# Sliding windows of 64 rows at stride 32: which blocks go through SBUF, and which ring moves the rest

## The chip, the cores and the metric

One core of a Trainium2 chip. The time is that of one execution on the device, in microseconds; every kernel was run several times and the median of its runs is given. A profile of an execution was taken as well; its span is some 2 us shorter than the time of the same execution.

## The reference, cut to what matters

```python
batch, length, dim = (32, 4096, 256)          # float32
window_size, stride = 64, 32
n_windows = (length - window_size) // stride + 1          # 127
for i in range(n_windows):
    start = i * stride
    result[:, i] = x[:, start:start + window_size]
```

Nothing is computed. A block is 32 rows of 256 floats, 32 KB; a batch has 128 blocks, and window w is blocks w and w+1. So each block is written twice, as the second half of one window and the first half of the next, except the first and the last of a batch. Input 134.2 MB, output 266.3 MB.

## The kernel before

There are two ways to fill the output. A *direct* copy goes from the input to the output, both in HBM: every output byte passes the DMA engines once, and is read from HBM and written to it. A *staged* block is loaded into SBUF once and stored from there twice: three passes of the engines for two output blocks, but one HBM read in place of two (the page's HBM line below bears this out). The kernel stages 11 of the 32 batches on the ACT ring, copies most of the others directly on the SP ring, 16 windows to a DMA, and leaves the edges of those to POOL's software ring, which starts when SP is nearly through. A ring is the queue of packets that one issuer (SP, ACT or POOL) fills, and the page has one queue for each. While two rings had work, the packet records count as many packets of the one as of the other: 2567 of SP's and 2574 of ACT's from 160 to 380 us in the first profile of before, whatever their sizes. One packet is called one *turn*, and a ring's turns here are its packets over 16 engines. The 4-byte packets are among them: 16 for each DMA of SP and ACT (3264 for SP's 204, 656 for ACT's 41). I take them for completions, as the trace has 16 semaphore updates for each DMA too (4272 for all 267).

```python
def windows(self, q, b, w0, n, half=None, piece=DIRECT):      # direct copy of n windows, or of one half of each
    blk = self.blk
    row = [1, 2 * blk if half is None else blk]
    h = half or 0
    return q.dma_start(out=self.oap((b * self.nw + w0) * 2 + h, [[2 * blk, n], row]),
                       in_=self.xap(b * self.nb + w0 + h, [[blk, n], row]), max_dma_last_dim=piece)
# ...
staged = [*range(1, B, 3)]                                    # 11 whole batches, 128 blocks each
# ...
edges = [(b, 0 if b - 1 in staged else 112, 15) for b in direct[:-1]]       # 20 software DMAs of 15 windows
# ...
st.run(ring_s)                                                # ACT: 6 loads, 12 stores, 5 loads, the other stores
for i, (b, w) in enumerate(sixteens):                         # SP
    sem = near if i == len(sixteens) - 2 else done
    second = turns - first_loads - stores
    loading = turns < first_loads or 0 <= second < loads
    share += 120 if turns < 16 or -8 <= second < 16 else 90 if loading else 18
    if share >= 120:                                          # "cut": one DMA for each half
        share -= 120
        turns += 4
        count(c.windows(ring_d, b, w, 16, 0), done)
        count(c.windows(ring_d, b, w, 16, 1), sem)
    else:
        turns += 3
        count(c.windows(ring_d, b, w, 16), sem)
# ...
ring_r.wait_ge(near, 16)                                      # POOL starts when SP's last copy but one has landed
```

The `share` counter decides which of SP's copies are cut into two DMAs. A cut adds 16 of the 4-byte packets, one turn more of SP's ring for the same bytes, and ACT's ring gets ahead: from 220 to 280 us ACT had 652 packets of 16 KB to SP's 442 of 32 KB in the first profile of before. This is how the kernel tunes the two rings against each other.

Of the kernel before, what the change touches and what calls it, by code (L numbers as in the profile page):

```python
# [8 lines left out]
DIRECT, IN, OUT = 32768, 16384, 16384  # L9


class Copier:


    def __init__(self, x, out, B, L, D, W, S, n_win):
        assert W == 2 * S and L % S == 0
        self.x, self.out = x, out
        self.B = B
        self.blk = S * D
        self.nb = L // S  # L20
        self.nw = n_win

    def xap(self, block, dims):
        return bass.AP(self.x.tensor, self.x.offset + block * self.blk, dims)

    def oap(self, half_window, dims):
        return bass.AP(self.out.tensor, self.out.offset + half_window * self.blk, dims)

    def windows(self, q, b, w0, n, half=None, piece=DIRECT):

        blk = self.blk
        row = [1, 2 * blk if half is None else blk]
        h = half or 0
        return q.dma_start(  # L34
            out=self.oap((b * self.nw + w0) * 2 + h, [[2 * blk, n], row]),
            in_=self.xap(b * self.nb + w0 + h, [[blk, n], row]),
            max_dma_last_dim=piece,
        )

    def columns(self, q, b, w0, n):  # L40

        part = self.blk // 8
        row = [1, part]
        return q.dma_start(  # L44
            out=self.oap((b * self.nw + w0) * 2, [[part, 16], [2 * self.blk, n], row]),
            in_=self.xap(b * self.nb + w0, [[part, 16], [self.blk, n], row]),
        )

    def load(self, q, t, b, c, rows):

        p, step, n, unit = rows
        return q.dma_start(
            out=t[p : p + (n - 1) * step + 1 : step, :],
            in_=self.xap(b * self.nb + c + p // unit, [[step // unit * self.blk, n], [1, self.blk]]),
            max_dma_last_dim=IN,
        )

    def store(self, q, t, b, c, rows, half):


        p, step, n, unit = rows
        w = b * self.nw + c + p // unit - half
        return q.dma_start(
            out=self.oap(2 * w + half, [[2 * step // unit * self.blk, n], [1, self.blk]]),
            in_=t[p : p + (n - 1) * step + 1 : step, :],
            max_dma_last_dim=OUT,
        )


class Staging:  # L70


    def __init__(self, c, tc, pool, dtype, items, bufs):
        self.c, self.items = c, items
        self.tiles = [pool.tile([128, c.blk], dtype, name=f"xb{i}") for i in range(bufs)]
        self.loaded = [tc.alloc_semaphore(f"loaded{i}") for i in range(bufs)]
        self.stored = [tc.alloc_semaphore(f"stored{i}") for i in range(bufs)]
        self.ended = tc.alloc_semaphore("ended")
        self.count = {sem: 0 for sem in (*self.loaded, *self.stored, self.ended)}
        self.after_load, self.after_store = {}, {}  # L80

    def issue(self, dma, sem):
        dma.then_inc(sem, 16)
# [1 line left out]

    def load(self, q, g):
        i = g % len(self.tiles)
        b, c, n = self.items[g]
        if self.count[self.stored[i]]:
            q.wait_ge(self.stored[i], self.count[self.stored[i]])  # L90
        step = 128 // n
        parts = [(k, 4, 32, 1) for k in range(4)] if g == 0 else [(0, step, n, step)]
        for rows in parts:
            self.issue(self.c.load(q, self.tiles[i], b, c, rows), self.loaded[i])
        self.after_load[g] = self.count[self.loaded[i]]

    def store(self, q, g):
        i = g % len(self.tiles)
        b, c, n = self.items[g]
        q.wait_ge(self.loaded[i], self.after_load[g])  # L100
        step = 128 // n
        parts, end = [((0, step, n, step), 0), ((0, step, n, step), 1)], []
        if g == len(self.items) - 1:

            parts = [((0, 1, 128, 1), 1), ((0, 1, 32, 1), 0)]
            end = [(96, 1, 32, 1)] + [(32 + k, 4, 16, 1) for k in range(4)]
        for rows, half in parts:
            self.issue(self.c.store(q, self.tiles[i], b, c, rows, half), self.stored[i])
        for rows in end:
            self.issue(self.c.store(q, self.tiles[i], b, c, rows, 0), self.ended)  # L110
        self.after_store[g] = self.count[self.stored[i]]

    def wait_stored(self, q, g):
        q.wait_ge(self.stored[g % len(self.tiles)], self.after_store[g])  # L114

    def run(self, q):
        bufs = len(self.tiles)
        for first in range(0, len(self.items), bufs):
            group = range(first, min(first + bufs, len(self.items)))
            for g in group:  # L120
                self.load(q, g)
            for g in group:
                self.store(q, g)


@with_exitstack
def kernel(
    ctx: ExitStack,
    tc: tile.TileContext,
    x: bass.AP,  # L130
    window_size: bass.AP,
    stride: bass.AP,
    out: bass.AP,
):
    nc = tc.nc
    W, S = int(window_size), int(stride)
    B, L, D = x.shape
    n_win = (L - W) // S + 1
    assert out.shape == (B, n_win, W, D)
    c = Copier(x, out, B, L, D, W, S, n_win)  # L140


    staged = [*range(1, B, 3)]
    items = [(b, -1 if b == B - 1 else 0, c.nb) for b in staged]
    place = {b: g for g, (b, _, n) in enumerate(items) if n == c.nb}
    direct = [b for b in range(B) if b not in staged]
    pool = ctx.enter_context(tc.tile_pool(name="xb", bufs=1))
    st = Staging(c, tc, pool, x.dtype, items, 6)
    ring_d, ring_s, ring_r = nc.sync, nc.scalar, nc.gpsimd
    done = tc.alloc_semaphore("done")  # L150
    near = tc.alloc_semaphore("near")
    rest = tc.alloc_semaphore("rest")
    total = {done: 0, near: 0, rest: 0}

    def count(dma, sem):
        dma.then_inc(sem, 16)
        total[sem] += 16



    sixteens = []
    for b in direct:
        w = 15 if b - 1 in staged else 0
        sixteens += [(b, w + 16 * j) for j in range((c.nw - w) // 16)]
    singles = [(B - 1, c.nw - 1, 1)]
    edges = [(b, 0 if b - 1 in staged else 112, 15) for b in direct[:-1]]
    last = B - 2
    edges.append((last, 112, 4))

    first_loads, loads, stores = 6 * 17, 5 * 17, 6 * 34  # L170
    turns = share = 0
    with tc.tile_critical():  # L172
        st.run(ring_s)

        for i, (b, w) in enumerate(sixteens):
            sem = near if i == len(sixteens) - 2 else done
            second = turns - first_loads - stores
            loading = turns < first_loads or 0 <= second < loads
            share += 120 if turns < 16 or -8 <= second < 16 else 90 if loading else 18
            if share >= 120:  # L180
                share -= 120
                turns += 4
                count(c.windows(ring_d, b, w, 16, 0), done)
                count(c.windows(ring_d, b, w, 16, 1), sem)
            else:
                turns += 3
                count(c.windows(ring_d, b, w, 16), sem)
            if i == len(sixteens) // 2:
                for b, w, half in singles:
                    count(c.windows(ring_d, b, w, 1, half, 2048), done)  # L190

        ring_r.wait_ge(near, 16)
        for b, w, n in edges:
            for k in (b - 1, b + 1):
                if k in place and b != last:
                    st.wait_stored(ring_r, place[k])
            count(c.windows(ring_r, b, w, n), rest)


        count(c.columns(ring_r, last, 116, 9), rest)  # L200
        st.wait_stored(ring_d, place[B - 1])
        count(c.columns(ring_d, last, 125, 2), done)
        total[st.ended] = st.count[st.ended]
        for sem, n in total.items():
            ring_d.wait_ge(sem, n)


# [33 lines left out]
```

## Time and profile before

| | before |
|---|---|
| median of 5 runs | 745.56 us (745.42 to 746.23) |
| span of the first profile | 749.4 us |
| span of a second profile (run e0_before, below) | 743.9 us |
| moved by the engines | 313.26 MB |

The first profile, on which the prediction rests, fell on an execution that took 751.2 us, longer than any timed one. Its page is shown in the prediction, with some of its waits (for whom: total us, times, longest); the HBM traffic, from the page: Two more lines of it matter later: the HBM traffic, from the page, and SP's last wait, from the waits of SP's queue (for whom: total us, times, longest).

```profile
HBM read 220.95 MB, written 267.09 MB: 651 GB/s over the span
```

```profile
SPq L172 <- POOLq L172: 1.7, 1, 1.7
```

A direct byte counts twice in the line, a staged one once for each pass: 174.83 MB went directly (q1 and q0), 46.14 were loaded and 92.27 stored, which makes 220.97 read and 267.10 written. The second lies at the very end: all data has landed (the last packet of the three rings ends at 745.8 us), and SP waits until POOL has finished a drain instruction (746.67 to 748.53 us in the trace).

### The profile page before, as it was taken

How to read it: one execution, taken by the hardware profiler on the slowest of the kernel's cores; microseconds unless marked ns; L12 is line 12 of the kernel's file. 1: busy time of each engine (PE TensorE's matmuls, PEld its weight loads, DVE VectorE, ACT ScalarE, POOL GpSimd, SP SyncE). 2: the span in 40 equal slices, each digit the busy share in tenths (PEclk: the TensorE clock that was granted, in tenths of full speed). 3: DMA queues.
4: the chain of work that ended last, by engine and by line, in shares of the span. 5: the costliest groups of instructions: out<-in, count | busy, mean ns of one | idle time of the engine just before them, and what ended most of it. 6: DMA issues, size and time to landing. Idle time of an engine off the chain costs nothing.

```text
span 749.4 us, 322 instructions
## 1 busy us (share of the span) xinstructions
POOL 12.8 (2%) x26
## 2 busy tenths in 40 slices
POOL 0000000000000000000000000000000000040100
DMA  8999999999999999999999999999999999999996
GB/s 360 401 427 429 427 429 428 434 423 418 420 424 423 418 424 415 422 427 427 414 427 417 429 432 429 430 422 430 429 423 421 423 421 419 425 426 423 431 409 262
DMA packets 18290, 313.26 MB, mean 418 GB/s; under 512 B 4336, under 2 KB 4336, under 8 KB 4528
## 3 DMA queue, kind: packets, MB, share of 16 engines
q1 hardware_dynamic: 8016, 154.32, 48.8%
q10 hardware_dynamic: 9104, 138.41, 44.0%
q0 software_dynamic: 1168, 20.51, 6.5%
q14 instruction: 2, 0.02, 0.0%
HBM read 220.95 MB, written 267.09 MB: 651 GB/s over the span
## 4 chain that ended last, share of the span: by engine, by line
another core or an unknown queue 92%; POOL 2%; issue 0%; POOLq 0%; SPq 0%
POOL out_dram L34 2%; POOL out_dram L44 0%; POOLq L236 0%; SPq L172 0%; POOLq L114 0%
## 5 line engine op out<-in xcount | busy, mean ns | idle before, releaser
L34 POOL DMA_DIRECT2D out_dram<-in_x_dram x21 | 12.0, 576 | 691.3 <-DMA out_dram<-in_x_dram 654.0
L44 POOL DMA_DIRECT2D out_dram<-in_x_dram x1 | 0.6, 581 | 0.0
L222 POOL MEMSET const-float32-0.0<- 128x1 f32 x1 | 0.1, 98 | 0.2 <-issue 0.2
L222 POOL MEMSET const-bfloat16-1.0<- 128x1 bf16 x1 | 0.1, 101 | 0.0
L222 POOL MEMSET const-float32-1.0<- 128x1 f32 x1 | 0.1, 98 | 0.0
L222 POOL MEMSET const-uint8-127<- 128x1 uint8 x1 | 0.1, 98 | 0.0
## 6 DMA issues: line engine op xcount, KB each, us to landing
out_dram<-in_x_dram SPq DMA_DIRECT2D x92, 1024.0 KB, 100.7
out_dram<-xb ACTq DMA_DIRECT2D x21, 4096.0 KB, 139.7
out_dram<-in_x_dram SPq DMA_DIRECT2D x110, 512.0 KB, 90.3
xb<-in_x_dram ACTq DMA_DIRECT2D x10, 4096.0 KB, 131.4
out_dram<-in_x_dram POOLq DMA_DIRECT2D x20, 960.0 KB, 38.5
xb<-in_x_dram ACTq DMA_DIRECT2D x4, 1024.0 KB, 15.7
out_dram<-xb ACTq DMA_DIRECT2D x2, 1024.0 KB, 113.4
out_dram<-xb ACTq DMA_DIRECT2D x4, 512.0 KB, 96.9
```

The source lines that it names most:

```text
L34: return q.dma_start(out=self.oap((b * self.nw + w0) * 2 + h, [[2 * blk, n], row]), in_=self.xap(b * self.nb + w0 + h, [[blk, n], row]), m ...
L44: return q.dma_start(out=self.oap((b * self.nw + w0) * 2, [[part, 16], [2 * self.blk, n], row]), in_=self.xap(b * self.nb + w0, [[part, 16 ...
L222: nc = _bacc.Bacc("TRN2", target_bir_lowering=False, num_devices=1)
```

## The change

It stages 64 inner blocks of 23 batches instead of all blocks of 11, so that no block is written twice. Two batches share a tile, on even and odd partitions. The outermost half windows next to the staged ranges go as "columns": 16 pieces of 2 KB for each of the 32 batches, one such DMA on each hardware ring. The last 14 windows of every batch go to the software ring, in DMAs of 14 or 7 windows.

```diff
-    def columns(self, q, b, w0, n):
-        part = self.blk // 8
+    def columns(self, q, b, w, half, n):
+        part = self.blk // 16
         row = [1, part]
         return q.dma_start(
-            out=self.oap((b * self.nw + w0) * 2, [[part, 16], [2 * self.blk, n], row]),
-            in_=self.xap(b * self.nb + w0, [[part, 16], [self.blk, n], row]),
+            out=self.oap(b, w, half, [[part, 16], [2 * self.nw * self.blk, n], row]),
+            in_=self.xap(b, w + half, [[part, 16], [self.nb * self.blk, n], row]),
         )
 ...
-    staged = [*range(1, B, 3)]
-    items = [(b, -1 if b == B - 1 else 0, c.nb) for b in staged]
+    far, pairs, n = B // 2, 11, 64
+    items = [(g, far, 1, n) for g in range(pairs + 1)]
+    alone = pairs
 ...
-        st.run(ring_s)
+        st.run(ring_s, lambda: count(c.columns(ring_s, 0, 0, 0, B)))     # after ACT's first 24 stores
 ...
-            share += 120 if turns < 16 or -8 <= second < 16 else 90 if loading else 18
+            share += 120 if turns < 16 or -8 <= second < 16 else 104 if loading else 83
 ...
+            if i == 84:
+                count(c.columns(ring_d, 0, n, 1, B))
         ring_r.wait_ge(near, 16)
-        for b, w, n in edges:
-            # (waits on staged stores, then a DMA of 15 windows)
+        for b in range(B):
+            w = n + 49
+            for m in (14,) if b % 2 else (7, 7):
+                c.remainder(ring_r, b, w, m).then_inc(rest, 16)
+                total_rest += 16
+                w += m
```

More of the change, by code (lines that the diff above doesn't have):

```diff
@@ L21, in __init__, with xap, oap, windows @@
         self.nw = n_win
-    def xap(self, block, dims):
-        return bass.AP(self.x.tensor, self.x.offset + block * self.blk, dims)
-    def oap(self, half_window, dims):
-        return bass.AP(self.out.tensor, self.out.offset + half_window * self.blk, dims)
-    def windows(self, q, b, w0, n, half=None, piece=DIRECT):
+    def xap(self, b, block, dims):
+        return bass.AP(self.x.tensor, self.x.offset + (b * self.nb + block) * self.blk, dims)
+    def oap(self, b, w, half, dims):
+        return bass.AP(self.out.tensor, self.out.offset + ((b * self.nw + w) * 2 + half) * self.blk, dims)
+    def windows(self, q, b, w, half=None):
         blk = self.blk
@@ L34, in windows, with remainder, load, store @@
         return q.dma_start(
-            out=self.oap((b * self.nw + w0) * 2 + h, [[2 * blk, n], row]),
-            in_=self.xap(b * self.nb + w0 + h, [[blk, n], row]),
-            max_dma_last_dim=piece,
-        )
-    def columns(self, q, b, w0, n):
-        part = self.blk // 8
+            out=self.oap(b, w, h, [[2 * blk, 16], row]),
+            in_=self.xap(b, w + h, [[blk, 16], row]),
+            max_dma_last_dim=DIRECT,
+        )
+    def remainder(self, q, b, w, n):
+        blk = self.blk
+        return q.dma_start(
+            out=self.oap(b, w, 0, [[2 * blk, n], [1, 2 * blk]]),
+            in_=self.xap(b, w, [[blk, n], [1, 2 * blk]]),
+            max_dma_last_dim=DIRECT,
+        )
+    def columns(self, q, b, w, half, n):
+        part = self.blk // 16
         row = [1, part]
         return q.dma_start(
-            out=self.oap((b * self.nw + w0) * 2, [[part, 16], [2 * self.blk, n], row]),
-            in_=self.xap(b * self.nb + w0, [[part, 16], [self.blk, n], row]),
-        )
-    def load(self, q, t, b, c, rows):
-        p, step, n, unit = rows
+            out=self.oap(b, w, half, [[part, 16], [2 * self.nw * self.blk, n], row]),
+            in_=self.xap(b, w + half, [[part, 16], [self.nb * self.blk, n], row]),
+        )
+    def load(self, q, t, b, c, k, step, n):
         return q.dma_start(
-            out=t[p : p + (n - 1) * step + 1 : step, :],
-            in_=self.xap(b * self.nb + c + p // unit, [[step // unit * self.blk, n], [1, self.blk]]),
+            out=t[k : k + (n - 1) * step + 1 : step, :],
+            in_=self.xap(b, c, [[step // 2 * self.blk, n], [1, self.blk]]),
             max_dma_last_dim=IN,
         )
-    def store(self, q, t, b, c, rows, half):
-        p, step, n, unit = rows
-        w = b * self.nw + c + p // unit - half
+    def store(self, q, t, b, c, k, n, half):
         return q.dma_start(
-            out=self.oap(2 * w + half, [[2 * step // unit * self.blk, n], [1, self.blk]]),
-            in_=t[p : p + (n - 1) * step + 1 : step, :],
+            out=self.oap(b, c - half, half, [[2 * self.blk, n], [1, self.blk]]),
+            in_=t[k : 2 * n : 2, :],
             max_dma_last_dim=OUT,
@@ L70, with __init__ @@
 class Staging:
-    def __init__(self, c, tc, pool, dtype, items, bufs):
-        self.c, self.items = c, items
+    def __init__(self, c, tc, pool, dtype, items, alone, bufs):
+        self.c, self.items, self.alone = c, items, alone
         self.tiles = [pool.tile([128, c.blk], dtype, name=f"xb{i}") for i in range(bufs)]
@@ L77, in __init__ @@
         self.stored = [tc.alloc_semaphore(f"stored{i}") for i in range(bufs)]
-        self.ended = tc.alloc_semaphore("ended")
-        self.count = {sem: 0 for sem in (*self.loaded, *self.stored, self.ended)}
-        self.after_load, self.after_store = {}, {}
+        self.count = {sem: 0 for sem in (*self.loaded, *self.stored)}
+        self.after_load = {}
     def issue(self, dma, sem):
@@ L87, in load @@
         i = g % len(self.tiles)
-        b, c, n = self.items[g]
         if self.count[self.stored[i]]:
             q.wait_ge(self.stored[i], self.count[self.stored[i]])
-        step = 128 // n
-        parts = [(k, 4, 32, 1) for k in range(4)] if g == 0 else [(0, step, n, step)]
-        for rows in parts:
-            self.issue(self.c.load(q, self.tiles[i], b, c, rows), self.loaded[i])
+        b, far, c, n = self.items[g]
+        step = 4 if g == 0 else 2
+        for k in range(step if g != self.alone else 1):
+            dma = self.c.load(q, self.tiles[i], b + far * (k % 2), c + k // 2, k, step, 2 * n // step)
+            self.issue(dma, self.loaded[i])
         self.after_load[g] = self.count[self.loaded[i]]
@@ L98, in store, with run @@
         i = g % len(self.tiles)
-        b, c, n = self.items[g]
         q.wait_ge(self.loaded[i], self.after_load[g])
-        step = 128 // n
-        parts, end = [((0, step, n, step), 0), ((0, step, n, step), 1)], []
-        if g == len(self.items) - 1:
-            parts = [((0, 1, 128, 1), 1), ((0, 1, 32, 1), 0)]
-            end = [(96, 1, 32, 1)] + [(32 + k, 4, 16, 1) for k in range(4)]
-        for rows, half in parts:
-            self.issue(self.c.store(q, self.tiles[i], b, c, rows, half), self.stored[i])
-        for rows in end:
-            self.issue(self.c.store(q, self.tiles[i], b, c, rows, 0), self.ended)
-        self.after_store[g] = self.count[self.stored[i]]
-    def wait_stored(self, q, g):
-        q.wait_ge(self.stored[g % len(self.tiles)], self.after_store[g])
-    def run(self, q):
+        b, far, c, n = self.items[g]
+        for half in (0, 1):
+            for k in (0, 1) if g != self.alone else (0,):
+                self.issue(self.c.store(q, self.tiles[i], b + far * k, c, k, n, half), self.stored[i])
+    def run(self, q, between):
         bufs = len(self.tiles)
@@ L123, in run, with wait_all @@
                 self.store(q, g)
+            if not first:
+                between()
+    def wait_all(self, q):
+        for sem in self.stored:
+            q.wait_ge(sem, self.count[sem])
 @with_exitstack
@@ L140 @@
     c = Copier(x, out, B, L, D, W, S, n_win)
-    staged = [*range(1, B, 3)]
-    items = [(b, -1 if b == B - 1 else 0, c.nb) for b in staged]
-    place = {b: g for g, (b, _, n) in enumerate(items) if n == c.nb}
-    direct = [b for b in range(B) if b not in staged]
+    far, pairs, n = B // 2, 11, 64
+    items = [(g, far, 1, n) for g in range(pairs + 1)]
+    alone = pairs
     pool = ctx.enter_context(tc.tile_pool(name="xb", bufs=1))
-    st = Staging(c, tc, pool, x.dtype, items, 6)
+    st = Staging(c, tc, pool, x.dtype, items, alone, 6)
@@ L149 @@
     ring_d, ring_s, ring_r = nc.sync, nc.scalar, nc.gpsimd
-    done = tc.alloc_semaphore("done")
     near = tc.alloc_semaphore("near")
     rest = tc.alloc_semaphore("rest")
-    total = {done: 0, near: 0, rest: 0}
-    def count(dma, sem):
-        dma.then_inc(sem, 16)
-        total[sem] += 16
-    sixteens = []
-    for b in direct:
-        w = 15 if b - 1 in staged else 0
-        sixteens += [(b, w + 16 * j) for j in range((c.nw - w) // 16)]
-    singles = [(B - 1, c.nw - 1, 1)]
-    edges = [(b, 0 if b - 1 in staged else 112, 15) for b in direct[:-1]]
@@ L167, with count @@
-    last = B - 2
-    edges.append((last, 112, 4))
-    first_loads, loads, stores = 6 * 17, 5 * 17, 6 * 34
+    total_rest = 0
+    done = tc.alloc_semaphore("done")
+    total = 0
+    def count(dma):
+        nonlocal total
+        dma.then_inc(done, 16)
+        total += 16
+    whole, split = [], []
+    for b in range(B):
+        whole += [(b, w) for w in range(n + 1, n + 49, 16)]
+        if b % far >= pairs and b != alone:
+            split += [(b, w) for w in range(0, n, 16)]
+    first_loads, loads, stores = 6 * 18, 5 * 18 + 9, 6 * 36
@@ L171 @@
     turns = share = 0
     with tc.tile_critical():
-        st.run(ring_s)
-        for i, (b, w) in enumerate(sixteens):
-            sem = near if i == len(sixteens) - 2 else done
+        st.run(ring_s, lambda: count(c.columns(ring_s, 0, 0, 0, B)))
+        k = 0
+        jobs = []
+        while k < len(whole) or split:
             second = turns - first_loads - stores
             loading = turns < first_loads or 0 <= second < loads
-            share += 120 if turns < 16 or -8 <= second < 16 else 90 if loading else 18
-            if share >= 120:
+            share += 120 if turns < 16 or -8 <= second < 16 else 104 if loading else 83
+            halves = share >= 120
+            if halves:
@@ L181 @@
                 share -= 120
-                turns += 4
-                count(c.windows(ring_d, b, w, 16, 0), done)
-                count(c.windows(ring_d, b, w, 16, 1), sem)
-            else:
-                turns += 3
-                count(c.windows(ring_d, b, w, 16), sem)
-            if i == len(sixteens) // 2:
-                for b, w, half in singles:
-                    count(c.windows(ring_d, b, w, 1, half, 2048), done)
-        ring_r.wait_ge(near, 16)
-        for b, w, n in edges:
-            for k in (b - 1, b + 1):
-                if k in place and b != last:
-                    st.wait_stored(ring_r, place[k])
-            count(c.windows(ring_r, b, w, n), rest)
@@ L200 @@
-        count(c.columns(ring_r, last, 116, 9), rest)
-        st.wait_stored(ring_d, place[B - 1])
-        count(c.columns(ring_d, last, 125, 2), done)
-        total[st.ended] = st.count[st.ended]
-        for sem, n in total.items():
-            ring_d.wait_ge(sem, n)
+            if split and (halves or k == len(whole)):
+                b, w = split.pop(0)
+                jobs.append(((b, w, 1), (b, w + 1, 0)))
+            else:
+                b, w = whole[k]
+                k += 1
+                jobs.append(((b, w, 0), (b, w, 1)) if halves else ((b, w),))
@@ new lines @@
+            turns += 2 + len(jobs[-1])
+        for i, job in enumerate(jobs):
+            for args in job:
+                dma = c.windows(ring_d, *args)
+                if i == len(jobs) - 2 and args is job[-1]:
+                    dma.then_inc(near, 16)
+                else:
+                    count(dma)
+            if i == 84:
+                count(c.columns(ring_d, 0, n, 1, B))
+        ring_r.wait_ge(near, 16)
+        for b in range(B):
+            w = n + 49
[3 more added lines that the diff above has]
+                w += m
@@ L209 @@
+        ring_d.wait_ge(rest, total_rest)
+        ring_d.wait_ge(done, total)
+        st.wait_all(ring_d)
 _INS = ['x', 'window_size', 'stride']
```

## The prediction

> **What bounds the kernel now.** The kernel only moves data, so I read the DMA lines of the page first, then the issues by size, then busy share by stretches of time, then the waits.
>
> ```profile
> span 749.4 us, 322 instructions
> DMA  8999999999999999999999999999999999999996
> GB/s 360 401 427 429 427 429 428 434 423 418 420 424 423 418 424 415 422 427 427 414 427 417 429 432 429 430 422 430 429 423 421 423 421 419 425 426 423 431 409 262
> DMA packets 18290, 313.26 MB, mean 418 GB/s; under 512 B 4336, under 2 KB 4336, under 8 KB 4528
> q1 hardware_dynamic: 8016, 154.32, 48.8%
> q10 hardware_dynamic: 9104, 138.41, 44.0%
> q0 software_dynamic: 1168, 20.51, 6.5%
> ```
>
> The 16 DMA engines are busy in nine tenths or more of every slice but the first and the last. The queue shares sum to 99.3% of the span, so there is almost no idle time to win: the time is the sum of what the packets cost. q1 is the SP ring (copies from input to output), q10 the ACT ring (loads into SBUF and stores from it), q0 the software ring of POOL.
>
> ```profile
> out_dram<-in_x_dram SPq DMA_DIRECT2D x92, 1024.0 KB, 100.7
> out_dram<-in_x_dram SPq DMA_DIRECT2D x110, 512.0 KB, 90.3
> ```
>
> These give the packet counts. SP moves 92 x 32 + 110 x 16 = 4704 packets of 32 KB. Its 8016 packets are those, 48 small ones and 3264 completion writes, which is 16 for each of its 204 DMAs. ACT's 9104 are 138.41 MB / 16 KB = 8448 packets and 16 x 41 completions. q0 has 608 packets of 32 KB, 144 of 4 KB and 416 of 4 B.
>
> Cost of a packet: q1's 48.8% of 16 x 749.4 us is 5851 us, some 1.23 us per 32 KB packet; q10's 44.0% over 8448 is 0.62 us per 16 KB. The trace's packet records, grouped by queue and size, give means of 1236 ns (32 KB, q1), 1248 ns (32 KB, q0), 624 ns (16 KB), 160 ns (4 KB), 84 ns (2 KB) and 9 ns (4 B); the medians of the first and third are 1213 and 611 ns. Twice 611 less 1213 is 9 ns, so cutting a packet in two costs about 9 ns: small packets are nearly free per byte.
>
> ```profile
> 40.00:160.00 120.00, 0.00 (x0) 1.00 1.01 429
> 160.00:430.00 270.00, 0.00 (x0) 1.00 1.00 422
> 656.50:658.70 2.20, 2.20 (x5) 1.00 1.03 439
> 736.00:742.00 6.00, 0.00 (x0) 1.00 0.91 383
> 742.00:746.00 4.00, 0.00 (x0) 1.00 0.30 124
> ```
>
> Columns: stretch, length, POOL busy, clock, DMA share, GB/s. With loads in the mix (40 to 160 us) the rate is 1.7% above that of the store stage. At 656.5 us the SP ring is empty and POOL's has not begun: ACT's ring alone keeps the engines full. The end is sharp: all engines run dry within about 6 us, so little is lost there either.
>
> ```profile
> POOL out_dram L34 <- DMA out_dram<-in_x_dram: 654.0, 1, 654.0
> SPq L44 <- DMA out_dram<-xb: 170.3, 1, 170.3
> ```
>
> POOL starts its 22 DMAs when SP's last copy but one has landed, at 654 us. These waits cost nothing while another ring has work.
>
> [...]
> - [...] 32768 B in 1213 ns on 16 engines is 432 GB/s. [...]
> - [...] SP has per engine 294 + 204 = 498 turns (leaving out the few small packets), ACT 528 + 41 = 569. When SP is through, ACT should have 71 left, and POOL has 38 + 9 + 26 = 73; so both should end together. In the records ACT's last packet ends at 745.1 us, POOL's at 745.8.
> - [...] Before, 20 x 15 + 4 = 304 = 19 x 16 rows, an even share. The engines' even end at 742 to 746 us fits; had one engine been left out it would have been idle for 38 x 1.24 = 47 us.
> [...]
>
> **The change, part by part.** Removed: 11 whole batches staged (128 blocks each), 23 blocks stored twice, the 4 KB columns, waits of POOL and SP on stores. Added: 64 inner blocks of 23 batches staged, two batches to a tile on even and odd partitions; two DMAs of 2 KB columns for the outermost half windows (32 batches x 16 pieces each), one on each hardware ring; 48 software DMAs of 7 or 14 windows.
>
> Bytes: loads 23 x 64 = 1472 blocks of 32 KB = 48.23 MB (before 46.14). Stores 96.47 MB. The output is 266.34 MB, each block once, against 267.09 MB written before. The engines move 266.34 + 48.23 = 314.57 MB against 313.26: +0.4%. The spared duplicates (0.75 MB) are outweighed by 2.1 MB more loading.
>
> Packets, from the program's order (132 copies of 16 windows on SP, 102 of them as two DMAs; 72 DMAs on ACT):
> - 32 KB on q1: 132 x 32 = 4224, 480 fewer, x 1236 ns = -593 us of one engine
> - 32 KB on q0: 16 x 28 x 2 = 896, 288 more, x 1248 = +359
> - 16 KB: (1472 + 2944) x 2 = 8832, 384 more, x 624 = +240
> - 2 KB: 1024, 1008 more, x 84 = +85
> - 4 KB: 176 fewer, x 160 = -28
> - completions: 235 + 72 + 48 = 355 DMAs for 267, 88 x 16 more, x 9 = +13
>
> The sum is +76 us of one engine, over 16 engines **+4.7 us**. All of it lies on the path, because the engines are full; nothing hides beside anything. No wait is worth anything by itself: those removed were covered by other rings.
>
> Is any ring left dry? Turns per engine: SP 264 + 32 + 235 = 531, ACT 552 + 32 + 72 = 656, POOL 56 + 48 = 104. When SP is through ACT has 125 turns left, about 111 of them stores: 111 x 0.624 = 69 us. POOL's are 56 x 1.248 = 70 us. So SP should end some 139 us before the end, near 611 us by the profile's clock, and POOL start there instead of at 654. POOL runs out 21 turns before ACT; then ACT drains alone for about 19 x 0.611 = 12 us. One ring alone ran at 439 GB/s above, so I put this at no loss. The balance of the software ring holds: 448 rows = 28 x 16. Tile reuse never starves ACT: tile 0's stores are over about 180 us in, its reload is asked for some 200 us later.
>
> **Rivals.**
> 1. *The columns are slow.* 64 packets per engine at 84 ns are 5.4 us of engine time. [...] Against it: every such packet alternates with a 16 or 32 KB packet of the other ring[...], and a 2 KB packet at 84 ns was seen in before[...]. I give +5 us or more one chance in seven.
> 2. *Staged packets get slower*[...]. For it: the first load of before, which steps by four partitions, has packets around 750 ns at 16 to 30 us, and that slice is the slowest full one (401 GB/s). Against it: at 4 to 16 us the same kind of load runs at 611 to 676 ns. If all 8832 packets took 2% more, +7 us, 757; at 5%, +17 us, the only way I see to "slower".
> 3. *Less writing helps.* HBM traffic falls from 488.0 to 484.4 MB, with a little more loading, which ran 1.7% faster than storing. 2 MB more loads and the store stretch without direct copies at the end are worth well under 1 us: 749.5.
> 4. *The end frays*: the software rows don't share out evenly[...]. Against it: the even end of the 15-row DMAs of before. One chance in thirty.
>
> **Range and chances.** 745.56 + 4.7 = 750.3, and a little for rivals 1 and 2 less rival 3: 750.8. The middle of the packet sum is safe to about 2 us; the risks lie upward, so 747.5 to 757. Faster by 2% would need under 730.7 us, that is 314.57 MB at over 430 GB/s with start and end included; the best slices reach 434, the mean 418. Slower by 2% is over 760.5 and needs rival 2 at 3% or rival 4.
>
> **What would show it.** Right: 314.6 MB; q1 about 139.5, q10 about 145.8, q0 29.4 MB; DMA digits of 9 up to the end; POOL first released near 607 to 612 us; q0 done some 10 us before the last stores; 2 KB packets near 84 ns; 16 KB packets near 624 ns. Wrong: a slice under 410 GB/s at about 390 to 430 us (ACT's columns) or where SP's stand (rival 1); q10's mean over 640 ns (rival 2); a last slice well under 262 GB/s with single engines still running (rival 4); a rate dip when ACT is alone, which would say that one ring can't fill the engines.

That the software ring's rows share out evenly over the engines is my estimate, from the even end of before at 742 to 746 us.

## The result, and the profile after

| | before | after |
|---|---|---|
| median of 5 runs | 745.56 us | 757.37 us (755.64 to 757.66) |
| ratio | | 1.0149 (95% interval 1.0135 to 1.0164) |

A ratio here is the mean time of one kernel's fast runs over that of the other's of the same rounds, so not quite the ratio of the medians quoted. The change is slower by 1.5%: inside "within 2%", as forecast, but 11.8 us where I had worked out 4.7, and 0.4 us above the range.

The page of the changed kernel, in the same order as in the prediction:

```profile
span 755.5 us, 411 instructions
DMA  8999999999999999999999999999999999999994
GB/s 364 426 425 429 431 428 433 430 426 433 435 433 428 430 434 429 431 433 431 429 344 394 430 432 432 428 434 429 435 430 433 429 424 415 420 425 421 422 397 146
DMA packets 21299, 314.62 MB, mean 416 GB/s; under 512 B 6320, under 2 KB 6320, under 8 KB 7344
q10 hardware_dynamic: 10496, 145.76, 45.7%
q1 hardware_dynamic: 8496, 139.48, 43.5%
q0 software_dynamic: 2304, 29.37, 9.8%
HBM read 218.10 MB, written 266.34 MB: 641 GB/s over the span
```

The bytes of each queue came as forecast, and so did the packets of q1 and q10. Three things did not. Slices 21 and 22 fell to 344 and 394 GB/s with the engines fully busy. The last two slices are 397 and 146, against 409 and 262. And q0 has 2304 packets; I had 896 + 768 = 1664.

Stretches of the same profile (from:to in us, length, POOL busy, clock, DMA share, GB/s):

```profile
380.00:390.00 10.00, 0.00 (x0) 1.00 0.98 325
390.00:400.00 10.00, 0.00 (x0) 1.00 1.07 323
410.00:600.00 190.00, 0.00 (x0) 1.00 1.00 431
728.00:735.00 7.00, 0.00 (x0) 1.00 1.04 372
735.00:740.00 5.00, 0.00 (x0) 1.00 1.03 354
740.00:745.00 5.00, 0.00 (x0) 1.00 0.72 236
```

In the second line the engines are fully busy (1.07) at 323 GB/s, so the packets themselves are slow. By the packet records, from 735 to 740 us q0 packets occupy 15.8 of the 16 engines, at 1507 ns for 32 KB: POOL's ring was alone, ACT's had run out. The forecast had it the other way round.

SP's last wait, and when POOL was released:

```profile
SPq L171 <- POOLq L171: 3.8, 1, 3.8
```

```profile
POOL out_dram L44 <- DMA out_dram<-in_x_dram: 603.1, 1, 603.1
```

The wait grew by 2.1 us; in the trace POOL's drain takes 3.99 us where it took 1.86 in the second profile of before. POOL's start, forecast for 607 to 612 us, was at 603.

The packet records, added up by queue and size, show where the time went. Each sum is divided by 16. "Before" is the second profile of that kernel (run e0_before, below), whose span, 743.9 us, is the typical one.

| packets | forecast change | before | after | change |
|---|---|---|---|---|
| 32 KB, SP | -37.1 us | 360.5 | 322.2 | -38.3 |
| 32 KB, POOL | +22.4 | 47.1 | 73.3 | +26.2 |
| 16 KB, ACT | +15.0 | 326.4 | 339.6 | +13.1 |
| 2 KB, SP and ACT | +5.3 | 0.1 | 9.0 | +8.9 |
| 4 KB | -1.8 | 1.8 | 0 | -1.8 |
| 4 B | +0.8 | 2.5 | 3.6 | +1.1 |
| sum | +4.7 | 738.4 | 747.6 | +9.2 |
| rest of the span | 0 | 5.5 | 7.9 | +2.4 |

Together 11.6 us, the difference of the two spans. The excess lies in the POOL packets (+3.8), the 2 KB packets (+3.6) and the last wait (+2.1); the large packets of SP and ACT gave 3.1 back.

### The profile page after: what moved, and what is told of

It is laid out like the page before. It is cut to its first block, busy times and chain, and to the rows that moved or that the text cites. A ratio compares the mean times of both kernels' runs of the same rounds, so it can differ in the third digit from the quotient of the medians.

```text
span 755.5 us, 411 instructions
## 1 busy us (share of the span) xinstructions
POOL 27.9 (4%) x52
## 3 DMA queue, kind: packets, MB, share of 16 engines
q0 software_dynamic: 2304, 29.37, 9.8%
## 4 chain that ended last, share of the span: by engine, by line
another core or an unknown queue 80%; POOL 4%; issue 0%; POOLq 0%; SPq 0%
POOL out_dram L44 4%; POOLq L240 0%; SPq L171 0%
## 5 line engine op out<-in xcount | busy, mean ns | idle before, releaser
L44 POOL DMA_DIRECT2D out_dram<-in_x_dram x48 | 27.8, 581 | 603.1 <-DMA out_dram<-in_x_dram 603.1
```

The costliest lines, as they stand in the source:

```text
L44: return q.dma_start(out=self.oap(b, w, 0, [[2 * blk, n], [1, 2 * blk]]), in_=self.xap(b, w, [[blk, n], [1, 2 * blk]]), max_dma_last_dim=D ...
```

## The experiments

The theories at the start: the columns cost (by their piece size, their pitch, or their meeting), and the end costs because POOL's ring outlasts ACT's. The rivals: these things are made up elsewhere, or the software ring is slow by itself.

### e0_before: the kernel before, again

No edit.

> The kernel before once more, unchanged. My prediction took packet means from one profile whose execution took 751.2 us, 5.6 us more than the median of the timed runs, while the profile of the changed kernel (757.6) is like its timed runs. Theory A (that profile was an untypically slow execution): the new profile has a shorter span, and its means lie nearer to 1213 and 611 ns than 1236 and 624, above all in the store stage at 160 to 380 us (more than the 421 GB/s it had). Rival B (the store stage of before is always slower than that of the changed kernel, because of what it stores): the profile again has about 421 GB/s there and the timed runs agree with 745.6 all the same.

Measured: 745.72 us, span 743.9, 1226 and 618 ns; on the same stretch of the store stage (220 to 280 us) 424 GB/s against 419 in the first profile. So the truth lies between A and B: my profile was of a slow execution, but the store stage of before is slower than that of the changed kernel (432) in both. e13 comes back to this.

### e1_rows: the columns as 32 KB rows

```diff
-            out=self.oap(b, w, half, [[part, 16], [2 * self.nw * self.blk, n], row]),
+            out=self.oap(b, w, half, [[2 * self.nw * self.blk, n], [1, self.blk]]),
```

(the same on the input side, and packets of up to 32 KB allowed)

> The changed kernel with its two column DMAs as 32 rows of 32 KB, the same bytes and the same 16 engines. Theory C (the 2 KB pieces cost about 5 us, seen as 344 and 394 GB/s in slices 21 and 22): 757.4 falls to about 752 to 753, and no slice at 380 to 420 us is under 415 GB/s. Rival D (the columns' slow stretch is given back later, as the rings drift apart): the dip goes, the time falls by under 1.5 us.

Measured: 758.01 us, ratio 1.0167; the rates of its 40 slices:

```profile
GB/s 371 416 431 429 431 426 432 426 431 429 440 428 432 430 432 429 433 430 428 438 326 386 437 429 429 433 430 433 429 434 427 432 430 406 426 416 424 432 391 156
```

Neither C nor D: the dip stayed, in slices 21 and 22. There are no small pieces here, so a dip doesn't need them. But the run has a flaw: each 32 KB row now comes from another batch, 4 MiB further on, and rows with that step were slow in e5 as well (some 190 GB/s for 336), so the run doesn't say what the pieces cost. ACT's 32 packets of this kind took 1739 ns on average, and SP's, while ACT's ring held nothing but stores, brought the rate down already:

```profile
382.00:386.00 4.00, 0.00 (x0) 1.00 0.90 225
```

### e2_fourteen: one software DMA for each batch

```diff
-            for m in (14,) if b % 2 else (7, 7):
+            for m in (14,):
```

> The changed kernel with every batch's last 14 windows as one software DMA, not two of 7 in the even batches. Theory E ([...]POOL's ring has 56 + 88 = 144 turns against ACT's 125 left, outlasts ACT's and then copies alone at 354 to 372 GB/s): 4-byte packets on q0 fall to 640, turns to 96, POOL ends before ACT, no stretch under 400 GB/s before the last few us, time down by 4 to 7 us to 751 to 753. Rival F (the software ring's packets are slow by themselves): q0's mean stays near 1309 ns and the time falls by under 2 us.

Measured: 752.2 us, ratio 1.0084 (1.0065 to 1.0102). The line of q0, then SP's last wait:

```profile
q0 software_dynamic: 1536, 29.36, 9.2%
```

```profile
SPq L171 <- POOLq L171: 2.5, 1, 2.5
```

The same bytes in 768 fewer packets. The 4-byte ones are 640, as forecast, and q0's 32 KB packets went from 1309 to 1226 ns, 4.6 us over 16 engines. In the records POOL now ends first, near 731 us, and ACT's stores run alone at 611 ns, full speed. Theory E holds and F falls: the very same software ring is fast (1226 ns) as long as ACT stores beside it. The median is 5.2 us lower; by the ratio it is 4.8. SP's last wait makes up 1.3 of that.

### e3_apart: the two column DMAs at different times

```diff
-            if i == 84:
+            if i == 40:
```

> The changed kernel with SP's columns after its copy 40, not 84, so that the two column DMAs no longer run at the same time. Theory G (it is the meeting of two rings of 2 KB pieces, with no large packet between them, that costs): the dip goes, 3 to 5 us gained, about 753. Rival H (each column DMA costs by its pieces and pitch wherever it stands): two smaller dips, 0 to 1.5 us gained.

Measured: 759.28 us, ratio 1.0185.

```profile
GB/s 369 419 429 431 429 431 421 434 425 428 430 433 428 431 434 430 437 429 437 393 329 391 431 429 429 431 431 431 433 431 425 424 436 418 418 425 422 420 405 180
```

Slower than the changed kernel, so G falls. But so does H. All 512 pieces of SP's column DMA, now beside ACT's stores at 187 to 210 us, took 84 ns, and slices 10 to 12 show nothing of them: pieces with the same pitch cost no more than these 84 ns on SP's ring. ACT's columns made a *longer* dip, in slices 20 to 22, now that SP sent 32 KB packets beside them. That asked for a new theory, K: it matters which ring holds the direct copies. ACT's ring is the only one that moves SBUF data. While it holds columns, all traffic is direct and every byte is both read from HBM and written to it. In e3 SP's 32 KB packets slowed as well during the dip (means of 1265 to 1503 ns in stretches of 3 us, for 1213 before it), so it isn't ACT's ring alone that is slow. The first line is e3 in its dip, the second the changed kernel while both rings hold columns:

```profile
374.00:398.00 24.00, 0.00 (x0) 1.00 0.95 326
```

```profile
388.00:392.00 4.00, 0.00 (x0) 1.00 1.06 249
```

Counting each byte twice, e3 has 652 GB/s at HBM, near the 672 that e5 will show. The changed kernel has at most 498 there, so for these few us K is not the whole cause: where pieces met pieces, the rate was lower still. Why (their size, their pitch or the meeting) stays open.

### e5_direct_sp and e6_direct_pool: direct copies alone

The whole output in direct copies of 16 windows, issued by SP alone, or by POOL alone; the last 15 windows of all batches in two DMAs at the end, one for each half.

> The whole output copied straight from the input by SP's ring alone in copies of 16 windows; nothing staged, nothing on another ring. It moves 266.3 MB. Theory I ([...]32 KB packets take about 1500 ns as at the end of the changed kernel): about 350 GB/s, 760 to 775 us. Rival J (it is the software ring that was slow there): 1213 to 1240 ns, about 430 GB/s, 620 to 630 us, faster than both kernels by far.

> The same copies on POOL's software ring alone. Theory I: as with SP's ring, within some per cent (760 to 790 us). Rival J: packets near 1500 ns here alone, over 760 us while SP's take 625.

Measured: 870.56 us on SP (ratio 1.1654), 891.41 us on POOL (one run). The rates in slices, SP first:

```profile
GB/s 313 330 336 336 338 336 335 330 336 336 339 335 332 335 333 342 336 335 330 336 336 338 336 335 333 335 338 330 333 336 339 335 235 191 190 184 185 200 205 158
```

```profile
GB/s 304 333 339 342 332 332 330 330 334 346 333 340 337 333 334 336 337 334 268 338 336 333 333 337 339 337 330 326 334 340 343 302 181 177 189 186 181 181 190 87
```

J falls: both kinds of ring run direct copies alone at about 336 GB/s, with busy engines (median packet 1576 and 1580 ns). Read and written together that is 672 GB/s at HBM. Theory I was right in kind, that direct copies alone are slow on either ring; that HBM is what holds them up is not shown. The times are over its forecast because the rate was 336 GB/s for its 350 and, above all, because of the last eight slices, near 190 GB/s. There the outermost step of each DMA is a batch, 4 MiB in the input, and for 32 KB rows this went with some 190 for 336 GB/s. The rows of e1 have the same step, which may be why it gained nothing.

### e7_sp_cols, e8_few_soft, e9_22: three steps towards a better version

e7 is e2 with both columns on SP's ring, beside ACT's stores, and fewer cuts (65 for 102) to keep the rings' ends together. e8 also takes four batches to a software DMA, with 85 cuts. e9 also stages 22 batches, not 23, with only 47 cuts.

```diff
-        st.run(ring_s, lambda: count(c.columns(ring_s, 0, 0, 0, B)))
+        st.run(ring_s, lambda: None)
-            share += ... else 104 if loading else 83
+            share += ... else 104 if loading else 24            # e8: 57, e9: 0
-            if i == 84:
+            if i == 40:
                 count(c.columns(ring_d, 0, n, 1, B))
+            if i == 60:
+                count(c.columns(ring_d, 0, 0, 0, B))
```

> e2_fourteen with both column DMAs on SP's ring, after its copies 40 and 60, where ACT's ring is storing; fewer SP copies are cut in two (65 for 102), so that ACT has about 96 turns left when SP is through, as many as POOL's 96. Theory K (what costs in the changed kernel's dip is that ACT's ring, the only one that moves SBUF data, holds copies from input to output, so that for 33 turns all traffic reads and writes HBM and runs at 300 to 336 GB/s): 2 KB packets at 84 ns, no slice under 410 GB/s at 370 to 420 us, 5 us less than e2_fourteen's 752.2, 746 to 748. Rival L (2 KB pieces or the 4 MiB pitch cost by themselves): two dips elsewhere and a time within 1.5 us of 752.

> e7 with the last 14 windows of four batches at a time in two software DMAs (one of the first halves, one of the second): 16 software DMAs for 32; POOL 76 turns, ACT 76 left (85 SP copies cut in two). Theory M (SP's last wait on POOL grows by about 0.079 us for each software DMA: 1.7, 2.5 and 3.8 us at 22, 32 and 48): 1.2 to 1.3 us, 1.2 us less than e7 in all, 745 to 746.5. Rival: the wait does not follow the number, or the 4-batch rows with their 4 MiB pitch are slow (q0 mean over 1250 ns), and e8 is no faster than e7.

> e8 with 22 batches staged in place of 23: 2.1 MB fewer loads, 312.5 MB in all, and 1 MB x 2 more of the stores as copies from input to output. Theory N (the engines, not HBM, bound the mixed stages): 2.1 MB at 430 GB/s, 4.5 to 5 us less than e8, about 741, faster than both kernels. Rival O (HBM binds first): 32 KB packets go from near 1221 up to 1240 ns and the gain is under 2 us.

Measured: 763.43, 762.78 and 763.11 us, where the kernel before took 755.09 on the same chip: ratios 1.0104, 1.0106 and 1.0107. This chip was slower for every kernel (the medians of the kernel before were 744.5 to 745.7 us on two of the chips and 753.7 to 755.1 on two others, so only ratios from one chip compare), and none of the three did what I had put down. The parts that can be read from the records:

- e7: all 1024 column packets took 84 ns, as K says, but the large ones took 1246 and 630 ns, and the gain was lost. (e13 and e14 take this apart.)
- e8: SP's last wait was 1.2 us, as M says. But q0's packets took 1336 ns for e7's 1274, 3.5 us over 16 engines, which ate it.
- e9: 1.0107 with 2.1 MB fewer bytes. N's gain of 4.5 to 5 us did not come, and SP's 32 KB packets took 1251 ns, as O says (e8: 1240; the kernel before, on another slow chip, e15: 1241). But e9 also has fewer cuts than e8, which costs by itself if theory Q below is right; so how much of the gain went to the cuts is not shown, nor that HBM took the rest.

### e12_fourteen and e11_no_act_cols: the dip by itself

e12 is e2 again. e11 is e12 without ACT's column DMA, and with SP's after copy 40.

```diff
-        st.run(ring_s, lambda: count(c.columns(ring_s, 0, 0, 0, B)))
+        st.run(ring_s, lambda: None)
-            if i == 84:
+            if i == 40:
```

> e2_fourteen again, unchanged, as the mate of the next run on the same chip. 1.008 x the kernel before, as the first time.

> e2_fourteen without ACT's column DMA, and with SP's columns after its copy 40, where they took 84 ns each in e3_apart. The first half window of each batch is not written, so the result is wrong on purpose; the mix of the other copies is untouched, other than in e7. Theory K (copies from input to output on ACT's ring leave HBM alone to carry all traffic): the dip near 380 to 405 us goes, all slices there over 415 GB/s, and the time falls by 7 to 8 us against e12 (1.05 MB less is 2.4 us, the dip 5.4). Rival P (the dip is the start of the second loads, or is made up elsewhere): only 2 to 3 us.

Measured: e12 750.72 us, ratio 1.0084, the same as the first time; e11 745.57 us, ratio 1.0012. The rates of e12, then of e11:

```profile
GB/s 362 430 425 433 434 430 424 429 434 429 439 424 433 430 432 430 440 424 432 428 369 391 432 431 428 433 433 432 425 439 429 432 425 430 436 419 431 432 417 203
```

```profile
GB/s 364 432 429 428 431 438 431 422 430 432 428 439 423 432 436 425 444 422 432 433 417 420 433 435 430 431 425 439 430 425 439 423 433 435 430 425 429 426 409 171
```

The dip is gone (417 and 420 for 369 and 391), so it is not the start of the second loads. The gain is 5.1 us, between the forecasts of K and P. The records say why: without the 33 turns of columns ACT's ring is nearly empty before POOL's is, and from 725 to 730 us POOL's packets take 1490 ns; their sum rises from 68.6 to 70.6 us.

```profile
725.00:730.00 5.00, 0.00 (x0) 1.00 0.96 338
```

Adding those 2.0 us, the columns and their dip were worth about 7 us, of which 2.4 are the bytes that e11 leaves out. The dip itself costs some 4 to 5 us. The rate gives about the same: e12 had 344 GB/s from 380 to 405 us, and (431 - 344) / 431 x 25 us = 5.0 us; the changed kernel had 334, which is 5.6 us.

### e10_pool_cols: what was learned, in one version

Columns as POOL's first DMAs, where ACT is storing; four batches to a software DMA; 95 cuts. (On POOL's ring the columns went as 512 packets of 4 KB, 159 ns each.)

```diff
-        st.run(ring_s, lambda: count(c.columns(ring_s, 0, 0, 0, B)))
+        st.run(ring_s, lambda: None)
-            if i == 84:
-                count(c.columns(ring_d, 0, n, 1, B))
-            share += ... else 104 if loading else 83
+            share += ... else 104 if loading else 72
+        c.columns(ring_r, 0, 0, 0, B).then_inc(rest, 16)
+        c.columns(ring_r, 0, n, 1, B).then_inc(rest, 16)
+        for b in range(0, B, 4):
+            for half in (0, 1):
+                c.remainder(ring_r, b, n + 49, half, 14, 4).then_inc(rest, 16)
```

> A correct version from what has been learned: the columns as POOL's first DMAs, where ACT is storing; 16 software DMAs of 14 windows of four batches; 95 SP copies cut in two, so the mix is near that of the changed kernel, and ACT has about 132 turns left for POOL's 142. If the terms add up (dip 5.4, tail 4, software DMAs 2.4): 11 to 12 us less than the changed kernel, level with the kernel before (ratio 0.998 to 1.003). If the four-batch rows are slow as e8's q0 (1336 ns) suggests: 3 us more, 1.004.

Measured: 748.2 us, ratio 1.0050 (1.0037 to 1.0062); correct. The slices:

```profile
GB/s 366 428 425 431 437 431 424 431 424 444 425 430 422 439 423 441 423 438 424 431 431 417 433 437 425 428 440 426 432 428 436 421 428 432 403 414 419 411 413 225
```

No dip, a short end, a last wait of 1.4 us. By the ratios it is 7.4 us better than the changed kernel and still 3.7 behind the kernel before. The second forecast, with slow four-batch rows, came closer: q0's packets took 1269 ns, against 1225 in e12, which is 2.5 us. No version tried beats the kernel before.

### e13_fewer_cuts, e14_sp_cols, e15_before: the cuts, the columns and the chip

e13 is e12 with e7's number of cuts and nothing else changed. e14 is e7 again, which differs from e13 only in where the columns stand. e15 is the kernel before.

```diff
-            share += ... else 104 if loading else 83
+            share += ... else 104 if loading else 24
```

> e12_fourteen with 65 SP copies cut in two in place of 102 (share 24 for 83 in the store stage); everything else the same. Theory Q (each completion takes a turn, so fewer cuts mean more input-to-output bytes beside each stored byte[...]): in the store stage at 160 to 380 us 32 KB packets of SP rise from 1213-1214 to over 1225 ns, the rate falls from 431 to about 423 GB/s, and the time rises to 1.011 to 1.014. Rival R (the mix does not matter; e7 to e9 were the chip): 1.007 to 1.009, packets as in e12.

> e7 once more, beside e13, which has the same number of cuts: the columns are all on SP's ring here. Theory K: no dip at 380 to 405 us, 3 to 5 us less than e13. Rival L: within 1.5 us of e13.

> The kernel before once more, for a profile on this chip: under theory Q about 421 to 428 GB/s in the store stage and 32 KB means of 1225 to 1236 ns, as with its other two profiles; under R as fast there as e12 was (1213 to 1215 ns).

Measured: 767.08, 760.65 and 753.07 us; ratios 1.0182, 1.0103 and 0.9999. The rates of e13, then of e14:

```profile
GB/s 371 410 430 426 420 422 425 427 416 418 422 413 423 419 425 413 424 418 419 420 418 316 354 435 431 416 424 428 428 425 408 430 427 418 418 424 412 414 431 220
```

```profile
GB/s 368 409 428 429 422 420 425 426 417 420 434 418 423 414 420 421 432 414 417 408 420 408 418 414 426 430 430 429 432 428 430 415 417 428 423 415 417 419 419 197
```

One stretch of the store stage, in e12, then e13, then e15:

```profile
220.00:280.00 60.00, 0.00 (x0) 1.00 1.01 432
```

```profile
220.00:280.00 60.00, 0.00 (x0) 1.00 1.00 418
```

```profile
220.00:280.00 60.00, 0.00 (x0) 1.00 1.01 422
```

- e14 against e13, on one chip: 1.0103 for 1.0182, some 6 us, for moving the columns off ACT's ring. e13's dip (316 and 354 GB/s) is gone in e14. K holds, L falls.
- e13 against e12, by their ratios: 1.0% slower. Some of this is a longer dip, as in e3 (the column DMAs no longer meet). The rest is the store stage: in that stretch SP's 32 KB packets took 1251 ns in e13 and 1213 in e12. With fewer cuts there is more direct copying beside each stored byte (449 packets for 432 in 60 us, against 633 stored ones for 718), and by theory Q this slows the packets. Counting direct bytes twice, the stretch has 663 GB/s at HBM in e13, 668 in e12, 666 in e15 and 661 to 669 in the two other profiles of before: all within 2% of e5's 672. I took HBM for the cause; these sums fit that but don't show it, as e12's packets run at 1213 ns with the same sum.
- The chip accounts for part: in the load stage (460 to 520 us) before's 32 KB packets took 1213 ns in e0 and 1220 in e15, on this chip. As e12 did not run there, I cannot say how much of 1213 to 1251 is the chip. Theory Q is supported by before, which has few cuts and was slower than e12 in this stretch on every chip (1235, 1250 and 1244 ns). On one chip alone there are only small steps: e7 (65 cuts) and e8 (85) had 418 and 422 GB/s from 160 to 380 us, e10 (95) and e12 (102) 431 and 432. At e8's step 37 cuts would be worth some 7 of the 13 GB/s between e13 and e12; this is an estimate, and leaves the rest to the chip.

## Why the prediction was wrong, point by point

The mechanism at large was right: the kernel is bound by the sum of its packets (the queue shares add up to 99.3% of the span before and 99.0% after), the change adds bytes and packets, and the time rises by less than 2%. Bytes, packet counts of the hardware rings, and POOL's start (603 us for "near 611") came as said. These steps failed:

- **"POOL 56 + 48 = 104. When SP is through ACT has 125 turns left ... POOL runs out 21 turns before ACT"**: the order in which the rings run dry. The term 48 was wrong: q0 had 1408 four-byte packets, 88 for each engine. Together with the 896 of 32 KB that is 2304 packets for 48 DMAs of 7 or 14 windows; e2 has 1536 for 32 DMAs of 14. Both are 48 packets for a DMA, whether 14 or 28 of them hold data, or three turns: 48 x 3 = 144. Why a DMA of fewer rows has more 4-byte packets (34 for 7 windows, 20 for 14, by these counts) is not shown. The hint was in the profile of before, where I wrote 416 for q0 and knew that 22 DMAs at 16 make 352, and I did not ask about the other 64. POOL outlasted ACT (data to 750.1 and 735.6 us); e2, which gives the turns 96, reverses the order and gains about 5 us, some 3.5 without the last wait.
- **"One ring alone ran at 439 GB/s above, so I put this at no loss."** That ring was ACT's, with stores, and for ACT it held (611 ns alone at the end of e2). But the ring left alone was POOL's, and a ring of direct copies alone runs at 336 GB/s (e5, e6). I had read the start of before and passed over it, SP alone at 262 GB/s with the engines 78% busy, which is 336 for full ones:

```profile
2.00:4.00 2.00, 0.00 (x0) 1.00 0.78 262
```

- **"2 KB: 1024, 1008 more, x 84 = +85."** Measured 130 and 150 ns on SP and ACT, with large packets slowed alongside, a dip of 4 to 6 us. Rival 1 had the size (+5 us or more) and the wrong cause, that the columns are slow wherever they stand: the same pieces, same pitch, took 84 ns on SP's ring beside stores (e3, e11, e14). The dip is there when ACT's ring stops moving SBUF data for 33 turns, and gone when it doesn't (some 5 us in e11, 6 us in e14 against e13); for the few us in which both rings hold pieces, there is something more that stays open.
- **"No wait is worth anything by itself."** SP's last wait on POOL grew from 1.7 to 3.8 us. Over five counts it follows the number of software DMAs at about 0.08 us each: 1.2, 1.4, 1.7, 2.5 and 3.8 us for 16, 18, 22, 32 and 48. It can't be carried further: e6 has 226, and POOL's drain took 8.1 us, not 18 (98 of them were issued after a pause of 341 us, and these alone would fit).
- **The packet means** came from an execution 5.6 us slower than the median, but this cost nothing: with e0's means (1226, 1240 and 618 ns) the sum is again +4.7 us. What the sum had wrong is that a packet keeps its time. SP's and ACT's large packets were faster than in before (1221 and 615 ns for 1226 and 618) and gave 3.1 us back, which fits theory Q (the changed kernel cuts more, and has 432 GB/s in the store stage). From 4.7 + 5 (dip) + 3.5 (end) + 2.1 (wait) = 15.3 to the measured 11.6 some 4 us are missing, and these 3.1 are most of them.
- **"With loads in the mix ... the rate is 1.7% above that of the store stage."** The numbers are right, but before also cuts far more of SP's copies while it loads. The changed kernel, which cuts in both stages, had 429 GB/s at 20 to 160 us and 431 in the store stage that follows. So loads are not shown to help (rival 3).

Rival 2 (slower staged packets) falls: the 16 KB packets took 615 ns on average, faster than before. Rival 4 falls: with DMAs of 7 rows 15.8 of the 16 engines still have work at 735 to 740 us.

## What to carry to other kernels

When a kernel only moves data, count two sums for every stretch of time: bytes through the engines, and bytes at HBM, where a copy from HBM to HBM counts twice (313.26 MB and 488.0 MB in before). In this kernel the ring that is the only one to move SBUF traffic was best given nothing else (some 6 us, e14 against e13), and best ran dry last (some 3.5 us, e2). The rings here went packet for packet (2567 to 2574 in 220 us), so count every packet of the profile, down to the 4-byte ones; a count that doesn't come out is a term missing from the sum.
